# Moving the tiles that TensorE reads to SBUF addresses that are multiples of 512 bytes

## The chip, the cores and the metric

The kernel runs on one core of one Trainium2 chip. That core has a matrix engine (TensorE, PE in the profile; its weight loads are listed apart, as PEld), a vector engine (DVE), a scalar engine (ACT), a general engine (POOL), a queue engine that issues the transfers (SP), and 16 DMA engines. SBUF is the on-chip memory: 128 partitions, and in each of them a tile is a run of bytes at the same address. PSUM is the memory that matrix products are written to. The metric is the device time of one execution in microseconds (us); the time of a kernel is the median of several executions.

## The reference

One layer of an encoder over 1024 tokens of width 1024, in float32. Cut to what matters:

```
h    = rmsnorm(x)
proj = h @ w_in                       # 1024 x 8096: latents, z, q/k/v of 24 heads, gates
a    = mla_attention(...)             # 8 heads, dense, 1024 x 1024 scores each
d    = dilated_mixture(q, k, v)       # 3 groups of 8 heads: windows of 129 keys at distance 1, 4, 16,
                                      # mixed with a softmax over the groups' denominators
y    = sigmoid(g_mla + b) * ((a * silu(z_mla)) @ w_o_mla) \
     + sigmoid(g_dil + b) * ((d * silu(z_dil)) @ w_o_dil)
out  = rmsnorm(x + y @ w_out)
```

## The kernel before, in words

Every large product is done in three passes. An operand X is kept as two tiles, X_h (rounded to the type float32r) and X_l = X - X_h, and `mm3` (L75 to L79) issues lh x rh, lh x rl and ll x rh into one PSUM tile. Each matmul has a weight load in front of it, so the program has nearly as many loads of 128 x 128 stationary values as matmuls. In the profile's notation `pj<-hT_h,w_h` the first operand is the moving one (up to 512 columns are streamed), the second the stationary one.

The work runs in these stages:

- **Latents and values** (`latent_proj`, `latents`, `dil_v`): first 416 moving columns of `wl_h`/`wl_l` against the transposed, normalised input `hT_h`/`hT_l`, then 256 columns of `w_h`/`w_l` against it.
- **Blocks** (`blocks`, L554): the queries and keys of the dilated heads, by a product scheme with seven instead of eight partial products. Four of the seven use block sums of the input (`s0` to `s3`, `_h` and `_l`) as the moving operand, three use `hT` itself; the stationary operand is always `w_h`/`w_l`. Each product is 12 matmuls of 512 columns. The order is written out by hand.
- **Dilated attention** (`dil_attention`, order by hand): scores `s_ps`, transposes of `p` through the identity in `consts`, products with the values (`av`). Between its steps `feed` issues pieces of `fillers`, the projections of z and of the gates (`pj<-hT,w`), so that TensorE has work while softmax steps run on the other engines.
- **Dense attention** (`mla_attention`): scores `s_mla<-op_b,op_a`, transposes of `p`, `av<-pt_h,op_c`; the rest of the fillers and the branch projections (`brd`, `brm` against `w`) are fed in between.
- **Output** (`output`): the last branch products, then `pj<-wout,m` and `pj<-wout,mg_l`, residual, norm, store.

**Where tiles lie.** A pool takes its tiles one behind the other; pools are stacked from the low end of SBUF (left) or, with `side="right"`, from the high end. A tile's size is rounded up to 32 bytes. Adding up the sizes gives these addresses modulo 512 for the tiles that TensorE reads: on the left the const pool ends at byte 5440, which is 10 x 512 + 320, so `op_a`, `op_b`, `op_c`, `pt_h`, `pt_l`, all `s` tiles, `mg_l` and `wout1` lie at 320; `lat_ss` adds 64 bytes, so `wl_h`/`wl_l` (their first column chunk), `uq`, `ukv` and `lat_h`/`lat_l` lie at 384; the small tiles `m_nm`, `m_den` and `m_d` of the pool `ap` add 320, so `brd`, `pt0`, the dense attention's `p` and, by `gap0`, `wout0` lie at 128; the dilated attention's `p` at 384. On the right the stack starts 32 bytes below a multiple of 512, and all tiles are multiples of 512 long, so `hT`, `w_h`, `w_l`, `brm` and `m1` lie at 480. The identity `consts` lies at 1184, which is 160 modulo 512.

Which later tile takes over whose bytes decides what a first write waits for (`reuse_waits="tile"`). The diff touches the functions printed here.

Of the kernel before, what the change touches and what calls it, by code (L numbers as in the profile page):

```python
# [10 lines left out]
F32 = mybir.dt.float32  # L11
# [3 lines left out]
ALU = mybir.AluOpType  # L15
# [22 lines left out]
DIL = (1, 4, 16)  # L38
# [16 lines left out]
class Net:  # L55
# [89 lines left out]
    def rsqrt_half(self, x, pool):  # L145

        v = self.nc.vector
        y, u = (pool.tile([128, 1], F32, name=f"rs_{c}") for c in "yu")
        self.nc.scalar.activation(out=y, in_=x, func=AF.Sqrt, scale=2.0)
        v.reciprocal(out=y, in_=y)  # L150
        v.scalar_tensor_tensor(out=u, in0=y, scalar=x, in1=y, op0=ALU.mult, op1=ALU.mult)
        v.scalar_tensor_tensor(out=y, in0=u, scalar=-1.5, in1=y, op0=ALU.add, op1=ALU.mult)
        return y
# [11 lines left out]
    def latent_proj(self, lp, wl, xp, pj):  # L165

        nc, a = self.nc, self.a
        v = nc.vector
        h = wl.tile([128, 8, 416], F32R, name="wl_h")
        l = wl.tile([128, 8, 416], F32R, name="wl_l")  # L170
        self.lat = lp.tile([128, 8, 448], F32, name="lat")
        self.lss = lp.tile([128, 2, 8], F32, name="lat_ss")
        nc.gpsimd.memset(self.lat[:, :, 384:448], 0.0)
        for half in range(2):
            ps = [pj.tile([128, 512], F32, name="pj") for _ in range(4)]
            todo = []
            for kc in range(8):
                self.load_x(half, kc, xp)
                if half == 0:
                    raw = wl.tile([128, 416], F32, name="wl_raw", bufs=3)  # L180
                    self.dma(raw, a["wl"][kc])
                    self.split(raw, h[:, kc], l[:, kc], nc.gpsimd if kc % 2 else v)
                for t in range(4):
                    todo.append((kc, t))
            if half:
                todo.sort(key=lambda x: x[1])
            for kc, t in todo:
                ts = slice(512 * half + 128 * t, 512 * half + 128 * t + 128)
                self.mm3(ps[t][:, :416], self.hTh[:, kc, ts], self.hTl[:, kc, ts], h[:, kc], l[:, kc], kc == 0, kc == 7)
            for t in range(4):  # L190
                i = 4 * half + t
                junk = xp.tile([128, 256], F32, name="x_junk", bufs=2)
                nc.scalar.activation(out=junk, in_=ps[t][:, 0:256], func=AF.Square, accum_out=self.lss[:, 0, i:i + 1])
                nc.scalar.activation(out=junk[:, 0:128], in_=ps[t][:, 256:384], func=AF.Square, accum_out=self.lss[:, 1, i:i + 1])
                v.tensor_copy(self.lat[:, i, 0:400], ps[t][:, 0:400])
                v.tensor_copy(self.lat[:, i, 416:432], ps[t][:, 400:416])
            if half == 0:
                v.tensor_scalar(out=self.hb, in0=self.hb, scalar1=0.5, scalar2=None, op0=ALU.mult)
# [511 lines left out]
    def mla_attention(self, ap, pp):  # L710
        nc = self.nc
        v = nc.vector
        for pair in range(4):
            num = [self.bp.tile([128, 512], F32, name=f"num{i}") for i in range(2)]
            nm = ap.tile([128, 2, 8], F32, name="m_nm", bufs=2)
            den = ap.tile([128, 2, 8], F32, name="m_den", bufs=2)
            for hh in range(2):
                h = pair * 2 + hh
                q = self.op.tile([96, 2, S], F32R, name="op_a", bufs=2)
# [53 lines left out]
    def mla_factors(self, pair, half, den, ap, pp):  # L773

        nc = self.nc
        v = nc.vector
        d = ap.tile([128, 2, 4], F32, name="m_d", bufs=2)
        v.tensor_scalar(out=d, in0=den[:, :, 4 * half:4 * half + 4], scalar1=2.0, scalar2=None, op0=ALU.mult)
        v.reciprocal(out=d, in_=d)
        tp = pp.tile([128, 512], F32, name="pt", bufs=NB_PT)  # L780
# [282 lines left out]
    def combine(self, pair, st, nums, ap, dx, pp):  # L1063
# [3 lines left out]
        o = {}  # L1067
# [7 lines left out]
        def wv(i, g):  # L1075
            w = o["w"][:, i]
            if g == 0:
                return w
            return w.rearrange("p h (m c) -> p h m c", c=DIL[g])
# [25 lines left out]
            nc.scalar.activation(out=o["w"][:, 0:3], in_=o["w"][:, 0:3], func=AF.Exp)  # L1105

        def factors():
            w = o["w"]
            dd = o["d"] = dx.tile([16, 3, 2, 64], F32, name="c_d", bufs=1)
            for g in range(3):  # L1110
                x = dd[:, g] if g == 0 else dd[:, g].rearrange("p h (m c) -> p h m c", c=DIL[g])
                v.tensor_tensor(out=x, in0=wv(g, g), in1=nat(1, g), op=ALU.mult)
            v.tensor_tensor(out=dd[:, 0], in0=dd[:, 0], in1=dd[:, 1], op=ALU.add)
            v.tensor_tensor(out=dd[:, 0], in0=dd[:, 0], in1=dd[:, 2], op=ALU.add)

        def quotients():
            w, dd = o["w"], o["d"]
            v.tensor_scalar(out=dd[:, 0], in0=dd[:, 0], scalar1=2.0, scalar2=None, op0=ALU.mult)
            v.reciprocal(out=dd[:, 0], in_=dd[:, 0])
            for g in range(3):  # L1120
                v.tensor_tensor(out=w[:, g], in0=w[:, g], in1=dd[:, 0], op=ALU.mult)
            self.dma(self.rr[pair].rearrange("y (x t) -> x y t", t=64), w[:, 0:3].rearrange("p g h t -> p (g h) t"))

        def spread(half, gs):
# [19 lines left out]
    def output(self, pp):  # L1144
        nc, a, tc = self.nc, self.a, self.tc
        v = nc.vector
        with tc.tile_pool(name="w3", reuse_waits="tile", bufs=1) as w3p, tc.tile_pool(name="mg", reuse_waits="tile", bufs=1) as mp, tc.tile_pool(name="wo", reuse_waits="tile", bufs=1) as wp:
# [3 lines left out]
            gates = [mp.tile([128, 512], F32, name="gate", bufs=5) for _ in range(5)]  # L1151

            o1 = [wp.tile([128, 8, 512], F32R, name=f"wout1_{c}") for c in "hl"]
            wp.tile([128, 80], F32, name="gap0")
            o0 = [wp.tile([128, 8, 512], F32R, name=f"wout0_{c}") for c in "hl"]
            wp.tile([128, 1024], F32, name="gap1")
            wo = o0, o1
# [33 lines left out]
            with tc.tile_pool(name="fin", reuse_waits="tile", bufs=2) as tp:  # L1191
# [4 lines left out]
                def first(t):  # L1196
                    x = tp.tile([128, D], F32, name="x_res", bufs=4)
                    self.dma(x, a["x"][128 * t:128 * t + 128, :])
                    return x, tp.tile([128, 3], F32, name="o_ss", bufs=4)

                def part(t, x, ss, i, lo, hi):
                    cs, ts = slice(lo, hi), slice(128 * t, 128 * t + 128)
# [15 lines left out]
                for t in range(8):  # L1218
# [4 lines left out]
                        i += t < 4  # L1223
                        part(t, x, ss, i, lo, hi)
                    y = tp.tile([128, D], F32, name="y_out", bufs=3)
                    rs = self.rsqrt_half(ss[:, i:i + 1], tp)
                    nc.scalar.mul(y[:, 0:512], x[:, 0:512], rs)
                    v.tensor_scalar(out=y[:, 512:D], in0=x[:, 512:D], scalar1=rs, scalar2=None, op0=ALU.mult)
                    self.dma(a["out"][ts, 512:D], y[:, 512:D])
# [2 lines left out]
    def run(self):  # L1232
        tc, nc = self.tc, self.nc
        with ExitStack() as ctx:
# [13 lines left out]
            self.constants(cp)  # L1248
            self.rs, self.cst = dt("s_rs", (8, 128)), dt("s_cs", (64, 2, S))
            self.rcol = cp.tile([128, 8], F32, name="rcol")  # L1250
            self.ht_pool = ExitStack()
            self.end_pools = ExitStack()
            self.brm_pool = ExitStack()
            self.wp = ctx.enter_context(tc.tile_pool(name="wp", reuse_waits="tile", bufs=2, side="right"))
            hp = self.ht_pool.enter_context(tc.tile_pool(name="ht", reuse_waits="tile", bufs=1, side="right"))
            self.R = hp.tile([128, S], F32, name="R")
# [46 lines left out]
            with tc.tile_pool(name="op", reuse_waits="tile", bufs=1) as self.op, tc.tile_pool(name="ap", reuse_waits="tile", bufs=1) as ap:  # L1303
                with tc.tile_pool(name="dx", reuse_waits="tile", bufs=1) as dx, tc.tile_pool(name="pj_b", reuse_waits="tile", bufs=2, space=PSUM) as self.pj, \
                        tc.tile_pool(name="at_s", reuse_waits="tile", bufs=1, space=PSUM) as self.sp, tc.tile_pool(name="av_b", reuse_waits="tile", bufs=2, space=PSUM) as self.avp:
                    self.pt0 = [dx.tile([128, 19 * 128], F32R, name=f"pt0_{c}") for c in "hl"]
                    for x in self.pt0:
                        nc.gpsimd.memset(x.bitcast(F32).rearrange("p (s q) -> p s q", q=128)[:, 0:19:9], 0.0)
                    with tc.manual_schedule():
# [89 lines left out]
```

## Time and profile before

| | |
|---|---|
| median of 3 executions | 1284.01 us (1281.53 to 1286.01) |
| span of the profiled execution | 1288.1 us, on a core with a mean granted TensorE clock of 0.988 |
| PE busy | 1236.5 us, 6957 matmuls; PEld 1073.3 us, as many loads |
| DVE, ACT, POOL busy | 752.6, 609.2, 506.7 us |
| DMA | 219.43 MB, 60.2% of 16 engines' span for the program's own queue |

The span of the profiled execution is 4.1 us longer than the median of the three times; its time with what lies around the span is not given apart. A matmul's duration in the profile is that of a pipelined instruction from its start to its end; several are in flight at once, so the time that a matmul costs a dense stream is the distance from its start to the start of the next one. The rows of the timeline give starts to 0.01 us, so a distance is read over many rows.

### The profile page before, as it was taken

The page shows a single profiled execution, that of the slowest core. Times are in us where ns is not written, and L with a number is a line of the kernel's source. Part 1 is how long each engine was busy: PE and PEld are TensorE (multiplying, and loading weights), DVE is VectorE, ACT ScalarE, POOL GpSimd, SP SyncE. Part 2 cuts the span into 40 slices and gives each one's busy share as a digit, 9 for nine tenths or more (in the row PEclk, how much of TensorE's full clock was granted, in tenths as well). Part 3 has the DMA queues.
Part 4 walks back from the last instruction along what each step waited for, and adds up shares of the span by engine and source line. Part 5 has one row for each costly group of instructions (what it writes and reads, how often), then busy time and mean ns, then how long its engine had stood idle before and what let it go on. Part 6 is the DMA issues. An engine that isn't in the chain of part 4 may idle for free.

```text
span 1288.1 us, 19688 instructions
## 1 busy us (share of the span) xinstructions
PE 1236.5 (96%) x6957; PEld 1073.3 (83%) x6957; DVE 752.6 (58%) x1368; ACT 609.2 (47%) x1276; POOL 506.7 (39%) x402
## 2 busy tenths in 40 slices
PE   8979999899999999999998999999999999998998
PEld 8978999788888877888887888888888888885786
DVE  7483524466556644566565664555566666668632
ACT  6523336344444326555464552455555555554322
POOL 2342218877767715435323041311211211247522
PEclk9989999999999998999998999999999999998999
DMA  9946674276456685988879797445346535135441
GB/s 328 251 157 251 237 286 143 85 181 160 129 140 155 146 218 153 212 197 221 207 202 235 185 229 190 155 118 134 127 115 172 143 97 150 58 107 184 159 148 49
DMA packets 134482, 219.43 MB, mean 170 GB/s; under 512 B 37160, under 2 KB 66672, under 8 KB 130480
## 3 DMA queue, kind: packets, MB, share of 16 engines
q1 hardware_dynamic: 134384, 218.17, 60.2%
q8 instruction: 55, 0.90, 0.3%
q14 instruction: 43, 0.35, 0.1%
HBM read 149.37 MB, written 68.75 MB: 169 GB/s over the span
## 4 chain that ended last, share of the span: by engine, by line
PE 69%; DMA 10%; issue 4%; DVE 3%; POOL 2%; SPq 2%; ACT 1%; DVEq 0%; POOLq 0%; ACTq 0%
PE pj L77 10%; PE pj L78 10%; PE pj L79 10%; PE pt L754 4%; PE av L763 2%; DMA op_a<-s_dk 2%; PE s_mla L77 2%; PE s_mla L79 2%; PE av L762 2%; PE s_mla L78 2%; DMA bc<-s_rr 2%; PE st_a L77 2%; PE st_a L79 2%; PE st_a L78 2%; PE st_c L79 2%
## 5 line engine op out<-in xcount | busy, mean ns | idle before, releaser
L84 POOL TENSOR_TENSOR w_l<-w_raw,w_h 128x512 fp32r<-128x512 f32 (+1 forms) x176 | 227.0, 1303 | 416.8 <-ACT w_h L83 360.2
L77 PE MATMUL pj<-hT_h,w_h 128*128 128x512 f32 x384 | 156.3, 407 | 0.0
L79 PE MATMUL pj<-hT_h,w_l 128*128 128x512 f32 x384 | 152.1, 396 | 0.0
L78 PE MATMUL pj<-hT_l,w_h 128*128 128x512 f32 x384 | 152.0, 396 | 0.0
L83 ACT CAST w_h<-w_raw 128x512 fp32r<-128x512 f32 (+1 forms) x176 | 104.3, 615 | 82.3 <-POOL w_raw L427 70.4
L84 DVE TENSOR_TENSOR pt_l<-pt,pt_h 128x512 fp32r<-128x512 f32 x128 | 88.0, 688 | 66.9 <-ACT pt_h L83 66.0
L83 ACT CAST pt_h<-pt 128x512 fp32r<-128x512 f32 x128 | 74.7, 585 | 79.7 <-PE pt L754 47.7
L77 PE MATMUL pj<-w_h,hT_h 128*128 128x256 f32 x384 | 109.2, 284 | 0.0
L78 PE MATMUL pj<-w_l,hT_h 128*128 128x256 f32 x384 | 109.0, 284 | 0.0
L79 PE MATMUL pj<-w_h,hT_l 128*128 128x256 f32 x384 | 108.9, 283 | 0.0
L740 DVE TENSOR_REDUCE m_nm<-s_mla 128x1 f32<-128x1024 f32 x64 | 78.2, 1222 | 27.0 <-PE s_mla L79 26.3
L870 DVE CUSTOM_DVE_ANT_0 p<-s_ps,masks 128x256 f32<-128x256 f32 x128 | 48.8, 419 | 73.6 <-PE s_ps L861 63.9
L877 ACT ACTIVATE p<-p,d_st 128x256 f32<-128x256 f32 x128 | 64.1, 502 | 54.3 <-DVE d_st L870 54.2
L79 PEld LDWEIGHTS pj<-hT_h,w_l 128*128 128x128 f32 x384 | 72.9, 190 | 15.8
L77 PEld LDWEIGHTS pj<-hT_h,w_h 128*128 128x128 f32 x384 | 73.4, 191 | 11.2
L78 PEld LDWEIGHTS pj<-hT_l,w_h 128*128 128x128 f32 x384 | 73.2, 191 | 11.3
L743 ACT ACTIVATE p<-s_mla,m_nm 128x1024 f32<-128x1024 f32 x64 | 71.8, 1122 | 18.6 <-PE pt L754 17.6
L754 PE MATMUL pt<-consts,p 128*128 128x128 f32 x512 | 78.1, 272 | 1.3 <-ACT p L743 1.3
L77 PEld LDWEIGHTS pj<-w_h,hT_h 128*128 128x128 f32 x384 | 73.7, 192 | 0.9
L78 PEld LDWEIGHTS pj<-w_l,hT_h 128*128 128x128 f32 x384 | 73.6, 192 | 0.8
L79 PEld LDWEIGHTS pj<-w_h,hT_l 128*128 128x128 f32 x384 | 73.7, 192 | 0.8
L762 PE MATMUL av<-pt_h,op_c 128*128 128x256 f32 x256 | 68.8, 289 | 0.0
(307 smaller groups left out, 3320.0 us busy)
## 6 DMA issues: line engine op xcount, KB each, us to landing
w_raw<-wt SPq DMA_DIRECT2D x48, 512.0 KB, 3.7
op_b<-s_dq SPq DMA_DIRECT2D x32, 512.0 KB, 8.4
gate<-s_gt SPq DMA_DIRECT2D x43, 256.0 KB, 2.9
s_dq<-dq_st SPq DMA_DIRECT2D x80, 128.0 KB, 2.4
s_dk<-dq_st SPq DMA_DIRECT2D x80, 128.0 KB, 2.4
s_dv<-dv_st SPq DMA_DIRECT2D x32, 256.0 KB, 4.1
s_gt<-zg_t SPq DMA_DIRECT2D x32, 256.0 KB, 3.7
w_raw<-wv SPq DMA_DIRECT2D x12, 512.0 KB, 3.6
```

The lines of the kernel that those rows point to most:

```text
L77: mm(out, lh, rh, start=start, stop=False, skip_group_check=skip)
L78: mm(out, lh, rl, start=False, stop=False, skip_group_check=skip)
L79: return mm(out, ll, rh, start=False, stop=stop, skip_group_check=skip)
L83: self.nc.scalar.copy(out=h, in_=raw)
L84: sub.tensor_tensor(out=l, in0=raw, in1=h.bitcast(F32), op=ALU.subtract)
L740: v.tensor_reduce(out=nm[:, hh, qb:qb + 1], in_=s, axis=AX.X, op=ALU.max, negate=True)
L743: nc.scalar.activation(out=p, in_=s, func=AF.Exp, bias=nm[:, hh, qb:qb + 1], accum_out=den[:, hh, qb:qb + 1])
L754: self.anchor = nc.tensor.transpose(pt[:, o:o + 128], P[b2][:, 128 * kc:128 * kc + 128], self.ident)
L762: nc.tensor.matmul(a_out, vv[:, kc], ph[:, s], start=kc == 0, stop=False)
L763: nc.tensor.matmul(a_out, vv[:, kc], pl[:, s], start=False, stop=kc == 7)
L870: nc.vector.tensor_tensor_reduce(out=p[:, c], in0=x["s"][:, c], in1=mask, op0=ALU.add, op1=ALU.min, scale=-0.125, scalar=3e38, accum_out=s ...
L877: nc.scalar.activation(out=p, in_=p, func=AF.Exp, scale=-1.0, bias=nm, accum_out=den)
```

## The change

It moves addresses, with little else:

- `edge_c` (64 bytes) and four 32-byte tiles of `rsqrt_half`, now in the const pool under new names, move the left stack by 192 bytes, to 5632 = 11 x 512.
- `edge_l` (448 bytes) fills up behind `lat_ss` to 512; `edge_d` (256 bytes) does so in front of the dilated attention's `d_st`.
- A new pool `edge` on the right, opened first, holds 480 bytes: one pad tile, and `m_nm`, `m_den`, `m_d` (from `ap`) and `o_ss` (from `fin`). It moves the right stack from 480 to 0 modulo 512, and `ap` loses its 320 odd bytes.
- `gap0` goes; `wout0` still lies on the bytes of `brd`.
- `factors` and `quotients` of `combine` work in place in `c_sn` instead of in a tile of their own, `c_d` (1536 bytes): the same number of DVE instructions of the same sizes.

`consts` stays where it was.

```diff
-        y, u = (pool.tile([128, 1], F32, name=f"rs_{c}") for c in "yu")
+        y, u = (pool.tile([128, 1], F32, name=f"rh_{c}", bufs=2) for c in "yu")
...
         self.lss = lp.tile([128, 2, 8], F32, name="lat_ss")
+        lp.tile([128, 112], F32, name="edge_l")
...
-            nm = ap.tile([128, 2, 8], F32, name="m_nm", bufs=2)
-            den = ap.tile([128, 2, 8], F32, name="m_den", bufs=2)
+            nm = self.ep.tile([128, 2, 8], F32, name="m_nm", bufs=2)
+            den = self.ep.tile([128, 2, 8], F32, name="m_den", bufs=2)
...
-        d = ap.tile([128, 2, 4], F32, name="m_d", bufs=2)
+        d = self.ep.tile([128, 2, 4], F32, name="m_d", bufs=2)
...
         def factors():
-            w = o["w"]
-            dd = o["d"] = dx.tile([16, 3, 2, 64], F32, name="c_d", bufs=1)
+            d = nat(1, 0)
             for g in range(3):
-                x = dd[:, g] if g == 0 else dd[:, g].rearrange("p h (m c) -> p h m c", c=DIL[g])
-                v.tensor_tensor(out=x, in0=wv(g, g), in1=nat(1, g), op=ALU.mult)
-            v.tensor_tensor(out=dd[:, 0], in0=dd[:, 0], in1=dd[:, 1], op=ALU.add)
-            v.tensor_tensor(out=dd[:, 0], in0=dd[:, 0], in1=dd[:, 2], op=ALU.add)
+                v.tensor_tensor(out=nat(1, g), in0=wv(g, g), in1=nat(1, g), op=ALU.mult)
+            for g in (1, 2):
+                y = d.rearrange("p h (m c) -> p h m c", c=DIL[g])
+                v.tensor_tensor(out=y, in0=y, in1=nat(1, g), op=ALU.add)
...
             o1 = [wp.tile([128, 8, 512], F32R, name=f"wout1_{c}") for c in "hl"]
-            wp.tile([128, 80], F32, name="gap0")
             o0 = [wp.tile([128, 8, 512], F32R, name=f"wout0_{c}") for c in "hl"]
...
-                    return x, tp.tile([128, 3], F32, name="o_ss", bufs=4)
+                    return x, self.ep.tile([128, 3], F32, name="o_ss", bufs=4)
...
-                    rs = self.rsqrt_half(ss[:, i:i + 1], tp)
+                    rs = self.rsqrt_half(ss[:, i:i + 1], self.cp)
...
             self.rcol = cp.tile([128, 8], F32, name="rcol")
+            cp.tile([128, 16], F32, name="edge_c")
+            self.cp = cp
...
+            self.ep = ctx.enter_context(tc.tile_pool(name="edge", reuse_waits="tile", bufs=1, side="right"))
+            self.ep.tile([128, 8], F32, name="edge")
...
                     self.pt0 = [dx.tile([128, 19 * 128], F32R, name=f"pt0_{c}") for c in "hl"]
+                    dx.tile([128, 64], F32, name="edge_d")
```

More of the change, by code (lines that the diff above doesn't have):

```diff
@@ L1107, in factors @@
         def factors():
-            w = o["w"]
-            dd = o["d"] = dx.tile([16, 3, 2, 64], F32, name="c_d", bufs=1)
+            d = nat(1, 0)
             for g in range(3):
-                x = dd[:, g] if g == 0 else dd[:, g].rearrange("p h (m c) -> p h m c", c=DIL[g])
-                v.tensor_tensor(out=x, in0=wv(g, g), in1=nat(1, g), op=ALU.mult)
-            v.tensor_tensor(out=dd[:, 0], in0=dd[:, 0], in1=dd[:, 1], op=ALU.add)
-            v.tensor_tensor(out=dd[:, 0], in0=dd[:, 0], in1=dd[:, 2], op=ALU.add)
+                v.tensor_tensor(out=nat(1, g), in0=wv(g, g), in1=nat(1, g), op=ALU.mult)
+            for g in (1, 2):
+                y = d.rearrange("p h (m c) -> p h m c", c=DIL[g])
+                v.tensor_tensor(out=y, in0=y, in1=nat(1, g), op=ALU.add)
         def quotients():
-            w, dd = o["w"], o["d"]
-            v.tensor_scalar(out=dd[:, 0], in0=dd[:, 0], scalar1=2.0, scalar2=None, op0=ALU.mult)
-            v.reciprocal(out=dd[:, 0], in_=dd[:, 0])
+            w, d = o["w"], nat(1, 0)
+            v.tensor_scalar(out=d, in0=d, scalar1=2.0, scalar2=None, op0=ALU.mult)
+            v.reciprocal(out=d, in_=d)
             for g in range(3):
-                v.tensor_tensor(out=w[:, g], in0=w[:, g], in1=dd[:, 0], op=ALU.mult)
+                v.tensor_tensor(out=w[:, g], in0=w[:, g], in1=d, op=ALU.mult)
             self.dma(self.rr[pair].rearrange("y (x t) -> x y t", t=64), w[:, 0:3].rearrange("p g h t -> p (g h) t"))
```

## The prediction, made before the result was known

> **What bounds the kernel now.** I read the page first, for the engine that fills the span and for the chain that ended last, then one table of windows by stage, then the timeline of TensorE inside the dense stretches. From the page:
>
> ```profile
> span 1288.1 us, 19688 instructions
> ...
> PE 1236.5 (96%) x6957; PEld 1073.3 (83%) x6957; DVE 752.6 (58%) x1368; ACT 609.2 (47%) x1276; POOL 506.7 (39%) x402
> ...
> PE 69%; DMA 10%; issue 4%; DVE 3%; POOL 2%; SPq 2%; ACT 1%; DVEq 0%; POOLq 0%; ACTq 0%
> ```
>
> TensorE holds 69% of the chain and the next one, DMA, 10%. So an edit that shortens the distance between matmuls can show in the time, and where it does is told by the windows (stretch, length, busy time and count of each engine, granted clock, DMA share, GB/s): the blocks, the dilated attention, the dense attention and the output; the last row is the part of the blocks from their first matmul on an `s` tile to their last one on `hT`, TensorE alone.
>
> ```profile
> 239.00:479.00 240.00, 240.00 (x1045) 195.25 (x1044) 147.37 (x237) 94.14 (x183) 161.15 (x127) 1.00 0.61 154
> 479.00:829.00 350.00, 331.97 (x1964) 290.94 (x1963) 204.39 (x517) 181.57 (x457) 125.97 (x110) 0.98 0.81 204
> 829.00:1116.00 287.00, 284.66 (x1664) 246.56 (x1663) 176.24 (x231) 154.51 (x280) 50.32 (x40) 1.00 0.44 124
> 1203.00:1288.00 85.00, 78.81 (x363) 64.60 (x361) 31.20 (x73) 23.95 (x57) 22.04 (x18) 0.99 0.26 90
> 235.91:460.67 224.76, 224.76 (x973) 1.00 0.58 148
> ```
>
> In the blocks TensorE is busy without a gap, and none of the other engines reaches 70%: what is saved per matmul there is saved. In the dilated attention 18 of 350 us are idle, and savings partly end in waits.
>
> Now the distances, from the timeline (start, duration, what). In each pair of rows the first and the last row of a run of matmuls stand; between them lie, in order, 10, 20, 5 and 29 more:
>
> ```profile
> 446.74 0.39 PE L77 MATMUL st_b<-hT_h,w_h 128*128 128x512 f32 x1
> 449.23 0.39 PE L79 MATMUL st_b<-hT_h,w_l 128*128 128x512 f32 x1
> ...
> 452.27 0.39 PE L77 MATMUL st_d<-s_h,w_h 128*128 128x512 f32 x1
> 457.17 0.39 PE L77 MATMUL st_a<-s_h,w_h 128*128 128x512 f32 x1
> ...
> 819.13 0.39 PE L78 MATMUL s_mla<-op_b,op_a 96*128 96x512 f32 x1
> 820.49 0.39 PE L78 MATMUL s_mla<-op_b,op_a 96*128 96x512 f32 x1
> ...
> 1195.74 0.40 PE L77 MATMUL pj<-wout_h,m 128*128 128x512 f32 x1
> 1202.74 0.40 PE L77 MATMUL pj<-wout_h,m 128*128 128x512 f32 x1
> ```
>
> The same 512 columns with a fresh weight load cost 2.49/11 = 226 ns on `hT` (480 modulo 512, weights 480), 4.90/21 = 233 ns on `s` (320, weights 480), 1.36/6 = 227 ns on `s_mla` (320, weights 320) and 7.00/30 = 233 ns on `wout0` (128, weights 480 and 320). Clock and shape are the same. What goes with the difference is the **offset between the moving and the stationary operand**: equal gives 227, unequal 233, and equal at 320 is no worse than equal at 480. That is the only sign in this trace that an address matters, and it speaks for a gain, a small one: 6.6 ns of 227.
>
> Two more readings limit it. A stream needs some matmuls to settle, and does so without any change of offset as well; and narrower matmuls do not show the effect (between the pairs lie 3, 10, 13 and 17 rows):
>
> ```profile
> 818.20 0.40 PE L77 MATMUL s_mla<-op_b,op_a 96*128 96x512 f32 x1
> 819.13 0.39 PE L78 MATMUL s_mla<-op_b,op_a 96*128 96x512 f32 x1
> ...
> 232.47 0.40 PE L77 MATMUL st_a<-hT_h,w_h 128*128 128x512 f32 x1
> 235.00 0.39 PE L79 MATMUL st_b<-hT_h,w_l 128*128 128x512 f32 x1
> ...
> 37.24 0.35 PE L77 MATMUL pj<-wl_h,hT_h 128*128 128x416 f32 x1
> 39.86 0.35 PE L79 MATMUL pj<-wl_h,hT_l 128*128 128x416 f32 x1
> ...
> 63.84 0.28 PE L78 MATMUL pj<-w_l,hT_h 128*128 128x256 f32 x1
> 66.00 0.28 PE L78 MATMUL pj<-w_l,hT_h 128*128 128x256 f32 x1
> ```
>
> At the switch from `hT` to `s_mla`, 818.20, four matmuls take 0.93/4 = 233 ns before the 227 sets in: 24 ns lost. But at 232.47, right after the clock has come up and with 480 on both sides all the time, eleven take 2.53/11 = 230 ns: 36 ns lost with no offset changed. And the 416 columns of `wl`, whose column chunks lie at 384, 0, 128 and 256 against weights at 480, cost 2.62/14 = 187 ns at each of these offsets; 256 columns cost 2.16/18 = 120 ns.
>
> **The change part by part.** After it, by the sizes in the diff, the left stack, the right stack and the odd pieces between them all come to 0 modulo 512, so moving and stationary operands have equal offsets in the blocks, the projections, the dense attention and the output. Still off are `consts` at 1184, the moving operand of the transposes, and the inner chunks of `wl`, 1664 bytes apart.
>
> (a) Blocks. The stretch holds 972 distances in 224.76 us; at 226.7 ns each they are 220.4 us. Gain at most 4.4, at least 0 if the offset is not the cause. I take 4.4, since the equal-offset rows just beside it show the rate that follows. All of it lies on the path: no gap on PE. What comes behind is the first load for the attention:
>
> ```profile
> 458.63 7.79 DMA op_a<-s_dk
> 466.48 15.47 DMA w_raw<-wt
> ...
> 450.15:456.03 5.88, 5.88 (x27) 1.00 0.26 64
> ```
>
> These two stand in the chain right behind the blocks. The window shows the DMA engines at 0.26 just before, so the loads wait for the blocks' last results and not for the queue, and move forward with them.
>
> (b) Output and the other mixed streams. The grouped rows (mean duration behind the bar) carry the counts; a duration exceeds the distance by a fixed 162 ns (389 stands with 227), so I compare durations with `st_b`'s 389:
>
> ```profile
> L78 PE MATMUL pj<-hT_l,w_h 128*128 128x512 f32 x384 | 152.0, 396 | 0.0
> L78 PE MATMUL s_mla<-op_b,op_a 96*128 96x512 f32 x128 | 50.3, 393 | 0.0
> L77 PE MATMUL pj<-wout_h,m 128*128 128x512 f32 x120 | 47.4, 396 | 2.0 <-ACT wout_h L83 2.0
> L79 PE MATMUL pj<-wout_h,mg_l 128*128 128x512 f32 x120 | 47.2, 394 | 0.0
> L78 PE MATMUL pj<-brd_l,w_h 128*128 128x512 f32 x64 | 25.3, 396 | 0.0
> L77 PE MATMUL st_b<-hT_h,w_h 128*128 128x512 f32 x48 | 18.7, 389 | 0.0
> ```
>
> `wout`: (7 + 2 x 5) ns x 120 = 2.0 us, on a dense stream near the end; I take 2.0, bounds 0 and 2.4 (360 x 6.6). The fillers, the scores and `brd`, counting two of three passes since the first also waits behind transposes: 768 x 7 + 256 x 4 + 128 x 7 = 7.3 us at most. But they run in pieces of three to nine between transposes and 256-column products, where the 36 ns of settling come without a change of offset; so I take a quarter, 1.8, of which some 1.4 arrive past the idle of that stage. The transposes and the 416- and 256-column products: 0.
>
> (c) `combine` in place and the moved small tiles. On the DVE, strided and plain operands of this size cost the same:
>
> ```profile
> L1121 DVE TENSOR_TENSOR c_w<-c_w,c_d 16x128 f32<-16x128 f32 x12 | 3.8, 366 | 0.1
> L1112 DVE TENSOR_TENSOR c_d<-c_w,c_sn 16x128 f32<-16x128 f32 x12 | 3.5, 336 | 0.6 <-ACT c_w L1105 0.6
> ```
>
> Five instructions per pair change their strides: 20 x 0.03 us either way, 0.6 at most, taken as 0. `c_sn` is now held until the quotients, a few DVE instructions longer; its next load is a pair later, so nothing on SP's queue waits for it. The buffers in `edge` and the const pool have the counts they had. The pads move late tiles against the earlier tenants of their bytes by up to 512 bytes; adding up sizes, the block sums still lie over the latents' tiles, `brd` over `pt0` and `num`, `x_res` over `brm`, so no first write gets a new wait: 0.
>
> Sum: 4.4 + 2.0 + 1.4 = 7.8 us. Against the profiled execution that is 1288.1 to 1280.3; against the median of the three runs, 4.1 below that span, 1284.0 to **1276**. Own range: half of (a) and (b)'s `wout`, 3.2, gives 1281; with all 7.3 of the mixed streams, 13.7, it is 1270.
>
> **The rivals.** First: **nothing measurable**, 1284. The distances then differ by something that goes along with the tiles, such as their strides (`s` 2048 bytes per chunk, `hT` 4096), not by their offset; the 416-column rows, flat over four offsets, speak for it, the 24 ns at a mere switch between two well-settled streams against it. [...]
>
> Second: **a large gain**. Every 512-column distance has something fixed in it. While the granted clock was 0.50 (last row) the same stream ran like this, with five rows between the first two; the third row is the 256-column matmul two rows before them:
>
> ```profile
> 487.75 0.63 PE L77 MATMUL pj<-hT_h,w_h 128*128 128x512 f32 x1
> 490.31 0.63 PE L77 MATMUL pj<-hT_h,w_h 128*128 128x512 f32 x1
> ...
> 487.32 0.41 PE L860 MATMUL s_ps<-op_a,op_b 128*128 128x256 f32 x1
> ...
> 487.80:490.20 2.40, 2.40 (x7) 1.92 (x7) 2.07 (x6) 2.04 (x8) 2.40 (x3) 0.50 0.79 255
> ```
>
> 2.56/6 = 426.7 ns, half of which is 213.3, and for 256 columns (487.75 - 487.32)/2 = 215, half 107: at full clock both are 13 ns above the half. If those 13 ns are the price of operands that straddle a multiple of 512, as nearly every stationary tile here does, they go too: 13 ns x (6957 less some 1100 transposes and narrow products) = 76 us, and by the chain's 69% 53 us; with the 7.8, 1223, or 1250 if half of it goes. Against it: equal pairs at 320 and 480 straddle by quite different amounts and cost the same 227. [...]
>
> Third: **slower**. If operands that start in the same place settle less well at 0, at the 233 of `wout0`, the streams that are equal today lose what the others were to gain: 432 matmuls on `hT` in the blocks x 6.6 = 2.9 us, and some 1500 in fillers and scores at 4 ns, 6 us: 1293. It decides from the first `st_b` on. For it: nothing lies at 0 on both sides now. Against it: 320 and 480 both settle at 227.
>
> **How the numbers follow.** Forecast 0.46, nothing 0.26, large gain 0.13, slower 0.15. About 0.3%, 3.9 us, is what a measurement of this kernel tells from no change. The forecast's own range reaches inside it at 1281: 0.39 faster, 0.07 same. Nothing: 0.20 same, 0.03 to each side. Large gain: 0.13 faster. Slower: 0.13 slower, 0.02 same. Together 0.55, 0.29, 0.16. The range runs from 1252, short of the large gain, to 1292, which cuts the slower case in half: 0.2 is left out.
>
> **What would show it.** Right: runs on `s` and `wout` at 227, durations of 389 where 394 to 399 stood, the blocks' stretch at 220 us. The second rival: `st_b` below 227 and 256 columns below 120. The third: `st_b` above 227. The first: `s` still at 233. Fillers that settle at 227 from their first matmul would mean that I took too little in (b).

## The result, and the profile after

The changed kernel takes 1271.32 us (median of six, 1265.43 to 1275.92); the kernel before, on the same chip, 1283.15 us (1276.74 to 1287.33). The ratio is 0.9908 with a 95% interval of 0.988 to 0.9936, so 11.8 us less, and between 8.2 and 15.4. The forecast was 7.8 us less, 1276. A second measurement, told below, gives 0.9917 (0.989 to 0.9945).

The page of the kernel after, the rows that answer to those shown of before:

```profile
span 1269.0 us, 19689 instructions
...
PE 1227.3 (97%) x6957; PEld 1071.7 (84%) x6957; DVE 750.3 (59%) x1368; ACT 608.1 (48%) x1276; POOL 506.5 (40%) x402
...
PE 71%; DMA 12%; DVE 5%; issue 4%; SPq 3%; POOL 3%; ACT 2%; DVEq 0%; ACTq 0%; POOLq 0%
```

The instructions are the same in number on every engine that computes, and TensorE still bounds the kernel. Its busy time fell by 1236.5 - 1227.3 = 9.2 us, the span by 19.1. So in this pair of profiles about half of what was saved is saved in matmuls and half in waits; the medians show 11.8, so part of the 19.1 belongs to the two executions that were profiled and not to the kernels.

The blocks after, TensorE alone, from the first matmul on an `s` tile to the last on `hT` (stretch, length, busy, granted clock, DMA share, GB/s):

```profile
228.51:449.43 220.92, 220.64 (x974) 1.00 0.56 150
```

224.76 us have become 220.92. Grouped rows of the kernel after (count, busy us, mean ns of one, idle before):

```profile
L78 PE MATMUL pj<-hT_l,w_h 128*128 128x512 f32 x384 | 151.7, 395 | 0.0
L78 PE MATMUL s_mla<-op_b,op_a 96*128 96x512 f32 x128 | 50.3, 393 | 0.0
L77 PE MATMUL pj<-wout_h,m 128*128 128x512 f32 x120 | 46.6, 390 | 2.0 <-ACT wout_h L83 2.0
L78 PE MATMUL pj<-wout_l,m 128*128 128x512 f32 x120 | 46.5, 389 | 0.0
L79 PE MATMUL st_c<-s_h,w_l 128*128 128x512 f32 x96 | 37.4, 389 | 0.0
L78 PE MATMUL pj<-brd_l,w_h 128*128 128x512 f32 x64 | 25.1, 393 | 0.0
L78 PE MATMUL pj<-wl_l,hT_h 128*128 128x416 f32 x64 | 22.9, 363 | 0.0
L77 PE MATMUL st_b<-hT_h,w_h 128*128 128x512 f32 x48 | 18.7, 389 | 0.0
```

The row of `st_c` before the change:

```profile
L79 PE MATMUL st_c<-s_h,w_l 128*128 128x512 f32 x96 | 38.2, 398 | 0.0
```

`s` and `wout` stand at 389 and 390, where `st_b` stood and stands. In these rows the scores have not moved (393), the fillers went from 396 to 395 and `brd` from 396 to 393. Of the three only `brd` had its operands apart before, 128 against 480: the fillers read `hT` and `w` at 480 and the scores `op_b` and `op_a` at 320, so their own offsets were equal before the change as well as after it.

And the dilated attention, from the fillers behind the blocks to the last transposes, with all engines (PE, PEld, DVE, ACT, POOL, then clock, DMA share, GB/s); first the kernel before, then after:

```profile
475.90:788.12 312.22, 294.19 (x1793) 259.85 (x1792) 182.00 (x482) 167.68 (x434) 111.29 (x99) 0.98 0.84 208
```

```profile
464.61:770.36 305.75, 292.68 (x1794) 259.61 (x1793) 184.46 (x482) 167.62 (x434) 110.76 (x99) 0.98 0.82 211
```

This stage has become 6.5 us shorter, with only 1.5 us less of matmuls. That the stage would wait less was in no part of the sum.

### The profile page after: what moved, and what is told of

It is laid out like the page before. It is cut to its first block, busy times and chain, and to the rows that moved or that the text cites. A ratio compares the mean times of both kernels' runs of the same rounds, so it can differ in the third digit from the quotient of the medians.

```text
span 1269.0 us, 19689 instructions
## 1 busy us (share of the span) xinstructions
PE 1227.3 (97%) x6957; PEld 1071.7 (84%) x6957; DVE 750.3 (59%) x1368; ACT 608.1 (48%) x1276; POOL 506.5 (40%) x402
## 4 chain that ended last, share of the span: by engine, by line
PE 71%; DMA 12%; DVE 5%; issue 4%; SPq 3%; POOL 3%; ACT 2%; DVEq 0%; ACTq 0%; POOLq 0%
PE pj L77 12%; PE pj L79 11%; PE pj L78 11%; PE pt L755 4%; SPq L73 3%; PE av L764 2%; PE av L763 2%; DMA bc<-s_rr 2%; PE s_mla L77 2%; PE s_mla L79 2%; PE s_mla L78 2%; PE st_c L77 2%; PE st_c L79 2%; PE st_c L78 2%; PE st_d L77 2%
```

## The experiments

Each kernel was timed against the kernel before, on the same chip, in five rounds, except where one time is given. A gain in us is worked out from the ratio, times the 1283 us of before. Offsets are addresses modulo 512 throughout.

### The changed kernel once more

No edit.

> The changed kernel once more, nothing edited, for a tighter ratio and a second profile. The blocks and the output together account for 6.0 us of the 11.8 between the medians; the rest stands in waits in the latents (5 us in the profile) and the dilated attention (6 us in the profile), in work that the change does not touch. My theory, that only the offsets of matmul operands matter: the blocks and the output keep their 389 ns, the ratio comes out between 0.992 and 0.996 (5 to 10 us), and the waits of the latents and the dilated attention differ from those of the first profile of the changed kernel by as much as those did from the kernel before. Rival, that the change also shortens those waits for good: ratio 0.991 or lower, and the wait of TensorE for lat_l on the Vector engine near 2.3 us again, not 6.5.

Measured: 1272.89 us, ratio 0.9917 (0.989 to 0.9945), 10.7 us less than before; between the two expectations. The waits tell more. The latents' stretch (first transposes of `lat` to the first product of `lat_h`) in the profiles of before, of after, and of the same kernel again:

```profile
55.70:89.69 33.99, 26.38 (x209) 25.84 (x207) 24.14 (x68) 8.97 (x17) 13.77 (x10) 0.90 0.54 167
```

```profile
56.43:85.31 28.88, 26.49 (x210) 26.12 (x207) 19.82 (x66) 8.86 (x17) 15.08 (x10) 0.94 0.55 185
```

```profile
55.77:89.73 33.96, 28.23 (x209) 27.29 (x207) 25.42 (x69) 9.19 (x18) 13.69 (x10) 0.85 0.51 173
```

The same kernel took 28.88 us there in one execution and 33.96 in another, part of it at a lower granted clock (0.94 and 0.85), so the 5.1 us of the latents in the first pair of profiles say nothing of the change. TensorE's waits for the Vector engine in this stretch were 7.6 us before, 2.3 after and 5.7 in the same kernel again. The dilated attention is another matter: it took 305.34 us in the second profile, beside 305.75 in the first and 312.22 before.

```profile
466.71:772.05 305.34, 291.58 (x1794) 259.36 (x1792) 183.93 (x482) 167.60 (x434) 110.79 (x99) 0.98 0.82 213
```

### Equal, or a multiple of 512?

On the kernel before, one pad, so that `s` starts at 480 as its weights do:

```diff
+        sp.tile([128, 40], F32, name="shift")
         self.sh = [sp.tile([128, 4, 512], F32R, name=f"s{i}_h") for i in range(4)]
```

> The kernel before with one pad of 160 bytes ahead of the block sums, so that the s tiles start at 480 modulo 512, as the weights and hT do; all else has the addresses of before. My theory, that equal offsets of the two operands decide and not the multiple of 512: matmuls on s take 389 ns (226 to 227 ns from start to start), the stretch of the blocks 220.5 us, and the time falls by 3 to 4.5 us. Rival, that both operands must start at a multiple of 512 bytes: s stays at 398 ns (233), the time stays the same within 1.5 us. Second rival, that the rate goes with the strides of s and not with its address: the same, 398 ns.

Measured: 1278.84 us, ratio 0.9964 (0.9942 to 0.9985), 4.6 us less. The blocks' stretch and a row on `s`:

```profile
227.09:448.07 220.98, 220.62 (x974) 1.00 0.59 150
```

```profile
L79 PE MATMUL st_c<-s_h,w_l 128*128 128x512 f32 x96 | 37.4, 389 | 0.0
```

All of the blocks' gain comes from one pad of 160 bytes, with not one operand of the blocks at a multiple of 512. It is the two operands' offset against each other that counts there.

### The same distance put back

The same line on the changed kernel: `s` at 160 against weights at 0.

> The changed kernel with a pad of 160 bytes ahead of the block sums: s at 160 modulo 512 against weights at 0, the distance that they had before (320 against 480), in the blocks alone. My theory: matmuls on s take 398 ns again (233 from start to start), the stretch of the blocks 224.5 us, and the time rises by 3 to 4.5 us against the changed kernel. Rival, that the 389 of the changed kernel comes from the weights or hT at 0 alone: s stays at 389 and the time too.

Measured: 1278.09 us, ratio 0.9956 (0.9936 to 0.9976): of the 10.7 us, 5.6 are left. The stretch and the row:

```profile
230.23:455.36 225.13, 225.13 (x974) 1.00 0.56 148
```

```profile
L78 PE MATMUL st_c<-s_l,w_h 128*128 128x512 f32 x96 | 38.1, 397 | 0.0
```

So the blocks are settled from both sides: 3.8 to 4.6 us in the trace, 4.6 and 5.1 in the times.

### The combine alone

The hunk of `combine` (`factors`, `quotients`) on the kernel before, nothing else:

```diff
-            dd = o["d"] = dx.tile([16, 3, 2, 64], F32, name="c_d", bufs=1)
+            d = nat(1, 0)
...
-                v.tensor_tensor(out=w[:, g], in0=w[:, g], in1=dd[:, 0], op=ALU.mult)
+                v.tensor_tensor(out=w[:, g], in0=w[:, g], in1=d, op=ALU.mult)
```

> The kernel before with one part of the change alone: the combine of the dilated attention in place, without the tile c_d, all addresses that TensorE reads as before but for what lies above that tile. My theory: no change, within 1.5 us of the kernel before, and matmul durations of before. Rival, that the shorter waits of the dilated attention in the profile of the changed kernel (some 6 us) come from the combine: 3 to 6 us less, and the waits of s_ps for op_a under 1 us each.

Measured: 1283.52 us, ratio 0.9996 (0.9979 to 1.0013). The combine brings nothing, as forecast, and its dilated attention waits as before.

### Both gaining stages put back

On the changed kernel `s` and both `wout` tiles at 160; `wout`'s pad is taken from `gap1`:

```diff
+        sp.tile([128, 40], F32, name="shift")
         self.sh = [sp.tile([128, 4, 512], F32R, name=f"s{i}_h") for i in range(4)]
...
+            wp.tile([128, 40], F32, name="gap0")
             o1 = [wp.tile([128, 8, 512], F32R, name=f"wout1_{c}") for c in "hl"]
             o0 = [wp.tile([128, 8, 512], F32R, name=f"wout0_{c}") for c in "hl"]
-            wp.tile([128, 1024], F32, name="gap1")
+            wp.tile([128, 984], F32, name="gap1")
```

> The changed kernel with the s tiles of the blocks and both wout tiles of the output at 160 modulo 512 against stationary operands at 0; all other addresses as changed. So the two stages that gained 6.0 us in the trace lose it again, and what is left is the rest of the gain. My theory, that the rest comes only from the 512-column fillers of the dilated attention (227 where 231 stood, 1.2 us) and the remainder of the waits was run to run: ratio to the kernel before between 0.997 and 1.001 (0 to 4 us faster, 1.2 expected). Rival, that the change also shortens the waits of the latents and the dilated attention for good: 4 to 6 us faster than before, ratio 0.995 to 0.997. In both, st_c on s takes 395 to 398 ns and wout 394 to 396.

Measured: 1277.78 us, ratio 0.9953 (0.9936 to 0.997): with the two forecast gains gone (blocks 225.16 us, `wout` 396 to 397 ns), the kernel is still 6.0 us faster than before. Here my theory of the first run fell. 1.2 us of fillers lie outside the interval of 3.9 to 8.2, and the dilated attention took 303.46 us, the shortest of all:

```profile
472.48:775.94 303.46, 290.24 (x1793) 257.89 (x1792) 185.26 (x482) 167.59 (x434) 110.77 (x99) 0.99 0.81 214
```

The times do not show the 2 us of `wout`: with `s` alone put back 5.6 us were left, with both 6.0, and intervals of some 2 us to each side are too wide for it. It rests on the trace, where the output, from the first to the last matmul on `wout`, took 89.99 us here and 87.34 in the change.

What differs in the dilated attention, when the packets of all transfers are grouped by size, is how long they take. The 16,864 packets of 256 bytes took 23.4 ns in the mean before and 19.9 after the change, those of 2048 bytes 113 and 104. The medians hardly differ (18 and 18 ns, 85 and 84); it is the slower half that got faster. Hence the new theory, which the last runs test.

### The identity of the transposes

`consts` split into the gains and the identity, the latter at 1536; pads and small tiles of the const pool go ahead of it:

```diff
-        c = cp.tile([128, 156], F32, name="consts")
-        self.dma(c, a["consts"])
+        c = cp.tile([128, 28], F32, name="gains")
+        self.dma(c, a["consts"][:, 128:156])
+        self.ident = cp.tile([128, 128], F32, name="consts")
+        self.dma(self.ident, a["consts"][:, 0:128])
```

> The changed kernel with the identity of the transposes, the one TensorE operand that the change leaves at 160 modulo 512, at 1536, a multiple of 512; the other constants in a tile of their own, loaded by a second transfer. Theory A: the fillers and scores of the dense attention do not settle (231 ns in the middle) because each group of transposes ends with an operand at another offset; then they come to 227 to 228 ns and the dense attention gets 2 to 4 us shorter. Theory B, mine: what unsettles them is the switch from 128 and 256 columns itself; durations stay at 393 to 395 and the time within 1.5 us of the changed kernel.

Measured: 1275.25 us, ratio 0.9933 (0.9907 to 0.9958), no better than the change alone. Over the 638 distances behind a 512-column filler or branch product in the dense attention that stay under 300 ns in all kernels, the mean is 230.1 ns, against 230.4 in the change and 230.4 before. The offset of the identity is not what keeps these streams from settling.

### Which distances cost

Three kernels, each timed once, all on the changed kernel: `s` at 32 and `wout` at 256; the same exchanged; `s` at 128 and `wout` at 64. In the first two `edge_l` is 96 bytes shorter, which gives `wl` its distances to `hT` of before. The edit of the first:

```diff
-        lp.tile([128, 112], F32, name="edge_l")
+        lp.tile([128, 88], F32, name="edge_l")
...
+        sp.tile([128, 8], F32, name="shift")
         self.sh = [sp.tile([128, 4, 512], F32R, name=f"s{i}_h") for i in range(4)]
...
+            wp.tile([128, 64], F32, name="gap0")
...
-            wp.tile([128, 1024], F32, name="gap1")
+            wp.tile([128, 960], F32, name="gap1")
```

> The changed kernel with the s tiles at 32 modulo 512 and the wout tiles at 256, against stationary operands at 0, and wl at 416, its distance to hT before. Which distances cost? Theory A, any distance but 0 costs the same: 233 ns for both (durations 395 to 398). Theory B, the cost grows with the distance: s at 228 or less, wout at 233 or more. Theory C, the period is 256 and not 512: wout at 227 and s at 233. The 416 columns of wl went from 187 to 190 ns with the change; at their old distances they go back to 187 if the distance between the operands sets that too, and stay at 190 if it is the weights at 0.

> The same with the two distances exchanged: s at 256, wout at 32. Theory A: 233 ns for both. Theory B: s at 233 or more, wout at 228 or less. Theory C: s at 227 and wout at 233. If the run before this one and this one disagree for the same distance, the number belongs to the tile and not to the distance.

> The changed kernel with s at 128 and wout at 64 modulo 512 against stationary operands at 0. So far 0 and 256 give 227 ns for 512 columns and 32 and 160 give 233. Theory A, that the period is 256: s at 233 and wout at 233. Theory B, that it is 128: s at 227 and wout at 233. Theory C, that it is 64, and 160 and 32 are bad only since they are odd multiples of 32: both at 227.

Single times: 1274.91, 1272.88 and 1274.95 us. A grouped row each from `s32_w256`, `s256_w32` and `s128_w64`, and in the last one the 256-column row of the output too:

```profile
L78 PE MATMUL pj<-wout_l,m 128*128 128x512 f32 x120 | 46.5, 389 | 0.0
...
L79 PE MATMUL st_a<-s_h,w_l 128*128 128x512 f32 x48 | 19.0, 395 | 0.0
```

```profile
L79 PE MATMUL st_c<-s_h,w_l 128*128 128x512 f32 x96 | 37.4, 389 | 0.0
...
L78 PE MATMUL pj<-wl_l,hT_h 128*128 128x416 f32 x64 | 22.8, 361 | 0.0
```

```profile
L79 PE MATMUL st_d<-s_h,w_l 128*128 128x512 f32 x48 | 19.0, 395 | 0.0
...
L78 PE MATMUL pj<-wout_l,m 128*128 128x256 f32 x16 | 4.4, 276 | 0.0
```

A distance of 256 bytes is as good as none, in the tile `wout` and in the tile `s`; 32 costs in both. Worked out from the start times of all kernels (means of the distances under 300 ns, in ns):

```
offset of moving against stationary   512 columns              256 columns (output)
0                                     226.7 (s), 226.7 (wout)  119.9
256                                   226.7 (s), 226.7 (wout)  119.9
32                                    233.5 (s), 233.4 (wout)  116.7
64                                    228.9 (wout)             113.3
128                                   233.2 (s)                -
160                                   234.2 (s), 234.3 (wout)  118.6
352 (96 modulo 256), before           233.6 (s)                -
```

So theory C of the first two runs, a period of 256, holds as far as the offsets tried go: 226.7 ns at 0 and at 256, 233 at 32. In the last run 128 costs in full, as its theory A has it, but none of its three theories has 64 right, which costs only 2 of the 7 ns (228.9).

The narrower products obey another order. The matmuls of 416 columns on `wl`, by the row of `wl_l`, went from a mean of 361 ns before to 363 with the change (187 to 190 ns from start to start); with their old distances they took 365 in `s32_w256` and 361 in `s256_w32`, so that the distance sets them too is not shown. The 256 columns of the output are slowest at 0 and 256 (119.9 ns) and gain 6.6 ns at 64 (113.3).

### The loaded operands off 512

The op tiles alone at 448 (`edge_c`, 64 bytes, goes, and each pool that lay behind it gets 64 bytes), and then at 480, with 32:

```diff
-            cp.tile([128, 16], F32, name="edge_c")
...
+        sp.tile([128, 16], F32, name="shift_sp")
...
+                            lp.tile([128, 16], F32, name="shift_lp")
...
+                ap.tile([128, 16], F32, name="shift_ap")
...
+            w3p.tile([128, 16], F32, name="shift_w3p")
```

> The changed kernel with the operands that both attentions load (op_a, op_b, op_c) at 448 modulo 512 and every other tile that TensorE reads at 0: the pad ahead of the op pool is taken out and put in again behind it. New theory, formed on the runs so far: what is left of the gain beside the matmuls (the kernel with s and wout at 160 is still 6.0 us faster than the one before) comes from the transfers, whose packets take less time where their SBUF side starts at a multiple of 512. In the dilated attention the packets took 276 us in sum over 16 engines before and 261 to 263 after; the load of 288 KB into op_a took 10.5 us from issue to landing before and 9.0 after, 128 KB into op_a 4.6 and 3.6. By it the loads go back to 10 us and over and 4.2 and over here, the waits above 500 ns of the dilated attention rise from 15 to 18 us or more, and the time comes to 1275 to 1278. Rival, that the transfers of the tiles on the right side (stores, gates, raw weights) or the combine brought it: the op loads stay at 9 and 3.6 us and the time at 1271 to 1273.

> As the run with the op tiles at 448, but at 480, which is no multiple of 64. Theory A, that 512 is the measure: packets and loads as at 448. Theory B, that multiples of 64 are the measure: at 448 the loads stay at 9 us, as after the change, and at 480 they take over 10.

Measured: at 448 1275.1 us, ratio 0.9928 (0.9905 to 0.9951); at 480 1277.3 us, once. The packets of the dilated attention took 275.0 and 278.9 us in sum over 16 engines, as before the change. Issues and loads (count, KB each, median us from issue to landing) in the kernels before, after, with op at 448 and at 480:

```profile
op_b<-s_dq SPq DMA_DIRECT2D x32, 512.0 KB, 8.4
...
op_a<-s_dk SPq DMA_DIRECT2D x16, 288.0 KB, 10.5
...
op_a<-s_dk SPq DMA_DIRECT2D x16, 128.0 KB, 4.6
```

```profile
op_b<-s_dq SPq DMA_DIRECT2D x32, 512.0 KB, 7.4
...
op_a<-s_dk SPq DMA_DIRECT2D x16, 288.0 KB, 9.0
...
op_a<-s_dk SPq DMA_DIRECT2D x16, 128.0 KB, 3.6
```

```profile
op_b<-s_dq SPq DMA_DIRECT2D x32, 512.0 KB, 8.4
...
op_a<-s_dk SPq DMA_DIRECT2D x16, 288.0 KB, 9.5
...
op_a<-s_dk SPq DMA_DIRECT2D x16, 128.0 KB, 4.5
```

```profile
op_b<-s_dq SPq DMA_DIRECT2D x32, 512.0 KB, 8.1
...
op_a<-s_dk SPq DMA_DIRECT2D x16, 288.0 KB, 10.7
...
op_a<-s_dk SPq DMA_DIRECT2D x16, 128.0 KB, 4.6
```

The loads are back, but for the 288 KB at 448, which I had expected over 10: its 9.5 us lie inside the 8.6 to 9.7 of the nine profiles with op at 0. TensorE's waits in the dilated attention (who waits for whom: us, times, longest), before, after, with `s` at 160 and op at 0, with op at 448 and with op at 480:

```profile
PE s_ps L860 <- DMA op_a<-s_dk: 5.4, 2, 3.0
PE pt L884 <- ACT p L877: 5.0, 1, 5.0
```

```profile
PE pt L885 <- ACT p L878: 3.9, 1, 3.9
PE s_ps L861 <- PE pt L990: 0.7, 1, 0.7
```

```profile
PE s_ps L862 <- DMA op_a<-s_dk: 5.2, 2, 2.9
PE pt L886 <- ACT p L879: 3.5, 1, 3.5
```

```profile
PE pt L886 <- ACT p L879: 5.2, 1, 5.2
PE s_ps L862 <- DMA op_a<-s_dk: 2.6, 3, 1.6
```

```profile
PE s_ps L862 <- DMA op_a<-s_dk: 6.6, 3, 4.1
PE pt L886 <- ACT p L879: 5.5, 1, 5.5
```

The wait that is put down to `op_a` does not follow the address from one profile to the next: with op at 0 it is nothing in the change but 5.2 us with `s` at 160, and with op at 448 it is 2.6. The first wait of the stage, that of `pt`, does: by the start times it takes 3.9 to 4.6 us in the nine profiles with op at 0, and 5.0 to 6.0 in the five with op elsewhere.

One execution is not enough for waits that vary by two or three us, so here are all profiles of the study (length of the stage and sum of its distances above 500 ns, from the matmuls' start times; sum of its packets' times, counted from the end of the blocks on; us):

```
op at   kernel                    length  waits  packets
320     before                    312.2   20.5   276.0
320     before, combine alone     314.4   22.9   275.3
320     before, s at 480          310.7   19.1   278.5
448     op at 448                 307.8   18.3   275.0
480     op at 480                 312.3   22.4   278.9
0       after                     305.7   14.6   262.7
0       after again               305.3   15.8   263.5
0       s at 160                  307.9   17.0   261.6
0       s and wout at 160         303.5   15.3   260.1
0       identity                  305.2   16.5   261.2
0       s at 32, wout at 256      305.2   16.7   262.3
0       s at 256, wout at 32      304.3   14.0   260.3
0       s at 128, wout at 64      306.2   16.0   261.8
0       right side at 32          305.9   16.9   262.9
```

Five profiles with the op tiles off 0 and nine with them at 0 do not overlap in waits (means 20.6 and 15.9, 4.8 us apart) nor in packets (277 and 262). Three of the five have nearly all other addresses as before the change too; the two that differ from it in the op tiles alone wait 18.3 and 22.4 us, 2.4 and 6.5 above the mean at 0. In length the two groups do overlap: 307.8 with op at 448, 307.9 with `s` at 160. Theory B, multiples of 64, fell: 448 is one. Whether 256 would do for the transfers, as it does for TensorE, no run tells. With op at 448 and 480 the fillers' distances rose a little as well (means 230.3 and 229.5 ns, 228.7 to 228.8 in the change), 1.1 and 0.5 us over 692 of them, so not all of the loss is in transfers.

### The right side off 512

```diff
-            self.ep.tile([128, 8], F32, name="edge")
...
+        sp.tile([128, 8], F32, name="shift_sp")
...
+            mp.tile([128, 8], F32, name="shift_mp")
...
-            wp.tile([128, 1024], F32, name="gap1")
+            wp.tile([128, 1016], F32, name="gap1")
```

> The other half: all tiles on the right side (weights, hT, the staging tiles of the stores, gates, raw weights, brm) at 32 modulo 512, with s, mg_l and wout at 32 too, so that the operands of the blocks, the fillers and the output stay equal; the op tiles and the others on the left at 0. Only brd and wl lie 32 off their weights. By the theory that the SBUF side of a transfer counts, the 2048-byte packets of the blocks, 137 ns in the mean before and 129 after, go back to 137, and the wait of the first transpose of the dilated attention, which hangs on the last stores of the blocks (5.0 to 6.0 us before, 3.9 to 4.3 after), to 5 us or more; the blocks themselves stay at 220.5 us, since TensorE sets them; in all 1 to 3 us slower than the changed kernel. Rival, that only loads count, or that the matmuls alone do: packets stay at 129 ns and the time at that of the changed kernel. The same run tells whether equal offsets are enough for TensorE at 32 as well: 389 ns.

Measured: 1271.44 us, ratio 0.9906 (0.9885 to 0.9927). As fast as the change; the first expectation missed. Blocks and output run at 389 to 390 and 394 to 395 ns, the latter because its first 15.5 us had a granted clock of 0.89; from start to start 226.7 and 226.9, so equal offsets do as well at 32 as at 0. The 8192 packets of 2048 bytes between the blocks' first and last matmul, stores from the right side, took 134 ns in the mean (134 after the change, 147 before; the expectation's 129 and 137 are from 180 to 475 us, a longer stretch, in which it is 128 here). With `s` at 480 on the kernel before, where the blocks' matmuls run as fast as after the change and the right side stands at 480, they took 146. The first wait of the dilated attention, which I had put down to the stores, is 4.3 us as with the change; with op at 448 and 480 it was 5.6 and 5.9 by the start times. So it goes with the op loads, which stand ahead of those stores on the queue, as in the kernel before (start, duration, what):

```profile
462.71 1.18 SPq L73 DMA_DIRECT2D op_a<-s_dk  x2
...
473.08 9.18 SPq L73 DMA_DIRECT2D s_dk<-dq_st  x8
```

So the right side's transfers were slower at 480 (146 and 147 ns) than at 0 and 32 (134), and 32 is no worse than 0. Being a multiple of 512 is not what they need. The 256-byte packets of the dilated attention, by the tiles' shapes nearly all loads into `op_b` and `op_c`, took 22.5 ns in the mean with the op tiles at 448, 23.4 at 320 and 19.9 at 0. What makes one offset slow and another not, no run tells.

## Why the prediction was right, and where it fell short

- **What bounds the kernel.** Right: TensorE, with savings per matmul showing in the time where it is busy without a gap.
- **Equal and unequal offsets.** The reading from four runs of the timeline, 227 against 233 ns, was the right cause, and both directions were shown (one pad brings the blocks' gain, the same pad on the changed kernel takes it away). Not right as put: unequal by 256 is as good as equal (226.7 ns), by 64 nearly so (228.9). And a matmul's own offset is not the whole of it: before the change 56 products of `wout1` with `mg_l` had equal offsets, 320 and 320, and took 233 ns all the same, among products with `m` that were 160 apart. Which pair of neighbours counts in such a mixed stream no run tells.
- **(a) Blocks**, 4.4 us: 3.8 and 4.2 us in the two profiles of the change, 4.6 and 5.1 in the times of the two pads.
- **(b) `wout`**, 2.0 us: the output's stretch, from the first to the last matmul on `wout`, went from 89.36 to 87.34 us, 2.0, in two executions with a granted clock of 1.00 there (windows of before and of after, as above); in the second profile of the change it took 88.96, with a clock of 0.90 in its first 16.5 us:

```profile
1192.17:1281.53 89.36, 89.36 (x407) 73.28 (x408) 39.63 (x79) 26.18 (x59) 31.34 (x22) 1.00 0.35 121
```

```profile
1175.06:1262.40 87.34, 87.34 (x408) 73.30 (x408) 39.59 (x79) 26.29 (x59) 31.29 (x22) 1.00 0.35 124
```

- **(b) Fillers, scores, `brd`**, a quarter of 7.3 us, 1.4 arriving: 692 distances behind fillers in the dilated attention fell by 0.8 us (159.1 to 158.3), the dense attention's 638 did not move (147.0 and 147.0). That they settle too slowly to profit was right; a quarter was still too much. The fillers' and the scores' own offsets were equal before the change too, 480 with 480 and 320 with 320, so by the prediction's own cause only what runs between them could bring a gain, and 6.4 of the 7.3 us were counted on them. Why they do not settle is open; the identity's offset is not the reason.
- **The 416- and 256-column products at 0.** "Narrower matmuls do not show the effect" was wrong. The four offsets of `wl` that I compared, 384, 0, 128 and 256 against 480, are all 32 off a multiple of 128 from their weights; that they were flat because they were alike in that is not shown: the change's distances, all multiples of 128, give 187 to 192 ns, by chunk. Cost here: up to 3 ns on 192 products, 0.6 us.
- **(c) Combine and moved tiles at 0.** Right for the combine (0.9996). The step that failed is in the moves: I followed who waits for whose bytes, and took every transfer's duration as given. **No term of the sum priced the SBUF address of a transfer.** The loads into the op tiles went from 10.5 to 9.0 us (288 KB) and from 4.6 to 3.6 (128 KB), and the waits of the dilated attention, which I had named only as the place where savings partly end, fell by 4.8 us in the means of all profiles.
- **The sum.** 4.2 (the blocks, in the middle of what the profiles show, 3.8 to 4.6) + 2.0 + 0.8 + 4.8 - 0.6 = 11.2 us, against 11.8 and 10.7 by the ratios. The terms that were forecast came to 7.0 of their 7.8; the missing one is more than the whole difference. That the result lies in the forecast's own range, 1270 to 1281, is luck: it lies at an end that was there for another reason, all 7.3 us of the mixed streams, and these brought 0.8.
- **The rivals.** Nothing: refuted. Large gain: refuted, `st_b` stays at 389 and 256 columns at 120. Slower: refuted, equal at 0 settles at 226.7, as at 32, 320 and 480.

What stays open: the transfers' share in the time itself. With op at 448 the ratio is 1.4 us above one measurement of the changed kernel and 2.6 above the other, and the intervals overlap; at 480 there is a single time, 1277.3 against 1271 to 1273. That the stage waits less with op at 0 is settled by fourteen profiles; how much of the 4.8 us is due to the op tiles alone, and that 4.8 us of waits are 4.8 us of time, is not. No run has `s`, `wout` and the op tiles put back at once, which would have to lose nearly all of the gain; so for some 4 to 6 us of it the cause is argued from waits and packets, not shown in the time. Nor is it known why an offset costs a matmul or a packet anything.

## What to carry to other kernels

Where matmuls of 512 float32 columns run back to back, compare the start addresses of moving and stationary operand modulo 256 before padding anything: here they took 226.7 ns at 0 and 256 and 233 to 234 at 160, and one pad of 160 bytes brought the 4.6 us of the blocks. An edit that moves tiles moves the ends of transfers too; group the packets by size, before and after, and look at the means and not at the medians (here 23.4 and 19.9 ns at 256 bytes, with 18 for both medians). And a wait in one profile is worth little until the same kernel's second profile shows it again: 5 us of the latents came and went with no edit at all.

## What the runs showed of the hardware that was not expected

- 512 columns take 226.7 ns at offsets 0 and 256 between the operands, 228.9 at 64, and 233 to 234 at 32, 128, 160 and 352; 256 columns go by another order, 119.9 ns at 0 and 256, 116.7 at 32 and 113.3 at 64. The 1152 products of 256 columns in the values' stage run at 120 ns; at 64 bytes apart, an estimate from 6.6 ns each is 7.6 us. No kernel here tried it there, and it may be too much: with op at 448 the `av` products of 256 columns had their operands 64 bytes apart, and their median distance was 117 to 118 ns, against 119 to 120 in the change.
- The 256-byte packets of the dilated attention took 19.9 ns in the mean with the op tiles at 0, and 22.5, 23.4 and 23.7 with them at 448, 320 and 480. Their median is 18 ns in all four, so the price falls on the slower ones (the slowest tenth took 26 to 27 ns or more at 0, 34 to 36 in the other three).
